# Two squared-ReLU MLPs in float32: block products by Strassen's algorithm in place of plain tiles

## The chip, the cores and the metric

One core of a Trainium2 chip runs the whole kernel in one launch. The metric is the time of one execution on the device, in microseconds (us). Of the kernel before there are three timed runs, and one more execution that was profiled.

## The reference

A decoder trunk of two layers on 1024 tokens of 1024 features, all in float32. Each layer has a mixer (layer 0: sparse attention beside a short convolution; layer 1: latent attention) and then an MLP, each inside two normalisations and a residual. The change concerns the MLP alone:

```python
x = x + rms_norm(mixer(rms_norm(x, g_mix_pre)), g_mix_post)
h = rms_norm(x, g_ffn_pre)                 # [1024 tokens, 1024]
u = jnp.square(jax.nn.relu(h @ w1))        # w1 [1024, 4096]
x = x + rms_norm(u @ w2, g_ffn_post)       # w2 [4096, 1024]
```

## The kernel before

**Products.** Every product is float32, made of three matmuls on rounded parts: a value v is split into hi, its copy in the rounded type fp32r (ScalarE, L258), and lo = v - hi (a subtraction on VectorE or GpSimd, L261). `mm3` (L266 to L269) then adds hi·hi, hi·lo and lo·hi into one PSUM region. So each product of two 128-row tiles has three matmuls, lines L267, L268 and L269, each 128 x 128 weights against up to 512 columns.

**Memory.** SBUF is cut into 25 pages of 8 KB per partition (class `Mem`, L35), from which all large tiles come; a tile that finds no page waits until another is freed. PSUM has two pools of two-bank tiles, `psS` (two buffers of [128, 1024]), and one-bank tiles, `psM` (three) and `psO` (one).

**Order.** The program is written in one thread of Python. A scheduler orders the instructions of TensorE, VectorE (DVE), ScalarE (ACT) and GpSimd (POOL) by its own estimate of when each is ready and how urgent it is; each engine then runs its list strictly in that order on the chip. SyncE (SP) issues the loads in the order of the program.

**Into the MLP.** `OutProj` (L781) multiplies a mixer's output by its projection, one block of 128 tokens at a time; `rest` (L824) adds the residual (L324, L325) and makes the next normalised block `xn` (L312). Two program steps later `put` (L834) gives it to `HN.put` (L336), which transposes it on TensorE (L341) and splits the transposed block into hi and lo. So the MLP's input is stored split, feature-major, before the MLP begins; `finish` (L840) does that for the last block. `Stream` (L271) loads and splits the weights of the MLP in tiles of [128, 1024] (512 KB), each tile once.

**The MLP** (`mlp`, L1105). The 4096 feed-forward columns are taken in 16 chunks of 256. For each chunk, `up` (L1111) makes two 128-column tiles for each half of the tokens: 8 row tiles of `w1` times 3 matmuls of 512 columns into a `psM` bank, then ReLU on ACT (L1118), the square on DVE (L1119) and the split into `at`. `down` (L1126) multiplies the chunk before by its rows of `w2` for each of the 8 token blocks into a `psS` tile of 1024 columns, and DVE adds it into the accumulator in SBUF (L1144). In the last chunks `down` takes two chunks at once and calls of a `tail` stand between its blocks: `tail0` (layer 0) normalises each finished block and starts layer 1's first projections (the `wd` products); `tail1` (L1470, layer 1) does the last residual row by row and writes the output. `tail1` calls the last block with `halves`, which evacuates its two halves apart (L1138), and finishes that row in halves (L1485 to L1493).

Of the kernel before, what the change touches and what calls it, by code (L numbers as in the profile page):

```python
# [21 lines left out]
P = 128  # L22
S = 1024
D = 1024
# [10 lines left out]
class Mem:  # L35
    """Pages of SBUF of 8 KB per partition; each serves tiles of one type, in quarters."""
# [96 lines left out]
def hybrid_kernel(ctx: ExitStack, tc: tile.TileContext, x, pos, g_mix_pre, g_mix_post, g_ffn_pre, g_ffn_post,  # L133
# [103 lines left out]
    def rope(eng, v, tb, off, n):  # L237
        """Rotates v [P, ..., 2n] of token block tb in place; off is where its table starts."""
# [32 lines left out]
    class Stream:  # L271
        """Weights in order of use: loads run ahead, then each is split into its parts."""
# [47 lines left out]
    def residual(src, tb, gain, xt, x_out, eng=None, queue=None):  # L320
        """x + rms(src) * gain of token block tb."""
# [8 lines left out]
    class HN:  # L330
        """Normalised activations, feature-major, in two parts."""
# [25 lines left out]
    # =========================================================== layer 0: mixer  # L357
# [88 lines left out]
    # start: normalise, transpose, first indexer chunk  # L446
# [19 lines left out]
    # key and weight columns of the indexer, feature-major, then token-major  # L466
# [314 lines left out]
    class OutProj:  # L781
        """Token-major product with weights [1024, 1024], residual and the next normalised activations;
        lhs_src(tb) gives the pieces of its transposed left side."""

        def __init__(self, weights, lhs_src, gpost, gpre, x_in, x_out, done, follow):
# [3 lines left out]
            self.hn, self.s, self.l, self.lag = HN(), {}, {}, []  # L789
# [15 lines left out]
        def product(self, tb):  # L805
# [6 lines left out]
            if tb == NB - 2:  # L812
                self.follow.load(2)
# [10 lines left out]
        def rest(self, tb):  # L824
# [3 lines left out]
            if tb >= NB - 1:  # L828
                self.follow.step(2 // 1)
# [717 lines left out]
```

## Time and profile before

| | us |
|---|---|
| median of three timed runs (lowest, highest) | 2734.79 (2731.08, 2738.48) |
| the profiled execution's own time: span from its first to its last instruction | 2734.3 |
| TensorE busy | 2654.1 (97%) |
| DVE busy | 1496.3 (55%) |
| ACT busy | 1112.1 (41%) |
| POOL busy | 824.5 (30%) |
| the six groups of MLP matmuls, 1024 each | 6144 matmuls |

The profile has six parts: busy time by engine; the span in 40 slices with the TensorE clock that was granted; the DMA queues; the chain of work that ended last; the costliest groups of instructions; and the DMA issues. The trace behind it can be asked for the instructions of one engine in order of time (the timeline), for tables of busy time by stretch (windows) and for groups by line. "Releaser" is what ended an engine's wait. A matmul's listed duration (389 ns) contains time in which the next one already runs, so the pace of matmuls is read from how many fit into a stretch.

### The profile page before, as it was taken

How to read it: one execution, taken by the hardware profiler on the slowest of the kernel's cores; microseconds unless marked ns; L12 is line 12 of the kernel's file. 1: busy time of each engine (PE TensorE's matmuls, PEld its weight loads, DVE VectorE, ACT ScalarE, POOL GpSimd, SP SyncE). 2: the span in 40 equal slices, each digit the busy share in tenths (PEclk: the TensorE clock that was granted, in tenths of full speed). 3: DMA queues.
4: the chain of work that ended last, by engine and by line, in shares of the span. 5: the costliest groups of instructions: out<-in, count | busy, mean ns of one | idle time of the engine just before them, and what ended most of it. 6: DMA issues, size and time to landing. Idle time of an engine off the chain costs nothing. (4 is left out here: it accounts for less than half of the span.)

```text
span 2734.3 us, 34579 instructions
## 1 busy us (share of the span) xinstructions
PE 2654.1 (97%) x13496; PEld 2214.3 (81%) x13496; DVE 1496.3 (55%) x2559; ACT 1112.1 (41%) x2107; POOL 824.5 (30%) x819
## 2 busy tenths in 40 slices
PE   7999999999999999999999999999999999999998
PEld 6887799766888888888888987777888888888887
DVE  5668999466543433333345478888652433433344
ACT  5554453576442212121224557888543222212122
POOL 4663255543022212122222233334112222222122
PEclk9999999999999999999999999999999999999999
DMA  3001110003421110111123341111331111110103
GB/s 113 24 32 47 62 63 17 1 1 111 136 77 54 39 62 31 62 48 46 54 77 108 127 156 52 34 47 48 108 116 54 41 53 54 39 62 31 62 31 131
DMA packets 67587, 171.58 MB, mean 63 GB/s; under 512 B 5904, under 2 KB 29968, under 8 KB 67424
## 3 DMA queue, kind: packets, MB, share of 16 engines
q1 hardware_dynamic: 60624, 145.19, 15.6%
q0 software_dynamic: 6656, 23.93, 2.3%
q8 instruction: 106, 1.74, 0.3%
q14 instruction: 57, 0.47, 0.1%
q10 hardware_dynamic: 144, 0.26, 0.0%
HBM read 138.95 MB, written 30.41 MB: 62 GB/s over the span
## 5 line engine op out<-in xcount | busy, mean ns | idle before, releaser
L261 POOL TENSOR_TENSOR w<-raw,w 128x1024 fp32r<-128x1024 f32 x128 | 307.4, 2401 | 1019.3 <-ACT w L258 1014.2
L1144 DVE TENSOR_TENSOR acc<-psS,acc 128x1024 f32<-128x1024 f32 x223 | 273.0, 1224 | 410.9 <-PE psS L269 410.4
L269 PE MATMUL psS<-w,at 128*128 128x512 f32 x1024 | 398.0, 389 | 2.1 <-DVE at L261 2.1
L267 PE MATMUL psS<-w,at 128*128 128x512 f32 x1024 | 398.8, 389 | 1.2 <-DVE acc L1138 0.8
L267 PE MATMUL psM<-hn,w 128*128 128x512 f32 x1024 | 398.5, 389 | 0.0
L268 PE MATMUL psS<-w,at 128*128 128x512 f32 x1024 | 398.4, 389 | 0.0
L269 PE MATMUL psM<-hn,w 128*128 128x512 f32 x1024 | 398.4, 389 | 0.0
L268 PE MATMUL psM<-hn,w 128*128 128x512 f32 x1024 | 398.3, 389 | 0.0
L258 ACT ACTIVATE w<-raw 128x1024 fp32r<-128x1024 f32 x132 | 139.7, 1059 | 618.3 <-PE psS L269 584.4
L1119 DVE SCALAR_TENSOR_TENSOR raw<-psM,raw 128x512 f32<-128x512 f32 x120 | 83.0, 691 | 302.4 <-ACT raw L1118 302.4
L269 PEld LDWEIGHTS psS<-w,at 128*128 128x128 f32 x1024 | 192.1, 188 | 42.8 <-DVE at L261 3.0
L267 PEld LDWEIGHTS psS<-w,at 128*128 128x128 f32 x1024 | 192.2, 188 | 41.7 <-DVE acc L1138 1.2
L268 PEld LDWEIGHTS psM<-hn,w 128*128 128x128 f32 x1024 | 192.2, 188 | 39.9
L269 PEld LDWEIGHTS psM<-hn,w 128*128 128x128 f32 x1024 | 192.2, 188 | 39.9
L268 PEld LDWEIGHTS psS<-w,at 128*128 128x128 f32 x1024 | 192.2, 188 | 39.7
L267 PEld LDWEIGHTS psM<-hn,w 128*128 128x128 f32 x1024 | 192.1, 188 | 39.8
L882 POOL TENSOR_SCALAR pr<-pr,tot 128x896 f32<-128x896 f32 (+7 forms) x181 | 133.5, 744 | 227.1 <-DVE tot L881 187.5
L1118 ACT ACTIVATE raw<-psM 128x512 f32<-128x512 f32 x120 | 71.8, 598 | 285.9 <-PE psM L269 285.9
L261 DVE TENSOR_TENSOR at<-raw,at 128x512 fp32r<-128x512 f32 x120 | 136.2, 1135 | 86.0 <-ACT at L258 86.0
L267 PE MATMUL psM<-wh,hn 128*128 128x256 f32 x576 | 159.3, 293 | 13.3 <-ACT tok L655 10.3
L269 PE MATMUL psM<-wh,hn 128*128 128x256 f32 x576 | 156.2, 288 | 0.0
L268 PE MATMUL psM<-wl,hn 128*128 128x256 f32 x552 | 150.4, 289 | 1.8 <-POOL wl L261 1.8
(707 smaller groups left out, 5509.0 us busy)
## 6 DMA issues: line engine op xcount, KB each, us to landing
raw<-in_w SPq DMA_DIRECT2D x128, 512.0 KB, 3.9
xt<-xs_d SPq DMA_DIRECT2D x15, 512.0 KB, 4.1
qtok<-q_d SPq DMA_DIRECT2D x8, 896.0 KB, 5.0
q_d<-qstage POOLq DMA_DIRECT2D x28, 224.0 KB, 2.6
xs_d<-xn POOLq DMA_DIRECT2D x12, 512.0 KB, 3.0
raw<-in_w_qkv SPq DMA_DIRECT2D x10, 512.0 KB, 4.2
xn<-in_x SPq DMA_DIRECT2D x9, 512.0 KB, 4.4
v_d<-vt POOLq DMA_DIRECT2D x8, 512.0 KB, 2.9
```

The costliest lines, as they stand in the source:

```text
L258: nc.scalar.activation(hi, src, AF.Copy)
L261: (lo_eng or nc.vector).tensor_tensor(lo, src, f(hi), op=ALU.subtract)
L267: nc.tensor.matmul(dst, lh, rh, start=start, stop=False)
L268: nc.tensor.matmul(dst, lh, rl, start=False, stop=False)
L269: nc.tensor.matmul(dst, ll, rh, start=False, stop=stop)
L882: nc.gpsimd.tensor_scalar(pt_, pt_, tot, 1.0, op0=ALU.mult, op1=ALU.mult)
L1118: nc.scalar.activation(r, m, AF.Relu)
L1119: nc.vector.scalar_tensor_tensor(r, m, 0.0, r, op0=ALU.max, op1=ALU.mult)
L1144: nc.vector.tensor_tensor(dst, s_, dst, op=ALU.add)
```

## The change

**What it does.** The 4096 columns are taken in four groups of 1024. In a group both products, up (tokens x features times features x columns) and down (tokens x columns times columns x features), are 1024 x 1024 x 1024, and each is cut into 2 x 2 blocks of 512 x 512. Seven products of sums and differences of blocks (the Winograd form of Strassen's algorithm) take the place of the eight plain block products. A block product n is 4 column tiles j by 4 contraction tiles q by 3 matmuls (L1277). Each of the 56 block products of a layer is a step: 4 groups of 7 up steps (order n = 1, 2, 6, 5, 7, 3, 4) and 7 down steps (n = 1, 5, 6, 3, 7, 2, 4). Steps alternate between two sets of four PSUM banks (three `psM` and `psO`; the two `psS`). Sums of products are kept by adding a later product into the same banks, and most products are evacuated in between.

The sums of blocks are formed in float32 on DVE by `comb` (L1109, 128 x 2048), and every combined block is split anew by `parts`: hi on ACT (L1102, two halves of 1024), lo (L1103, two halves) on POOL or DVE, by the table in `left` and `right`. So the MLP's input is not split by `put` any more: `Blocks` stores it transposed in float32 (copies L372). The seven splits of the MLP's input are made in group 0, on DVE, stored to DRAM by SP and read back for groups 1 to 3. The weights come in 1 MB tiles of [128, 2048]. The preparation of a step stands one step ahead of its product in the program. In the last step (n = 4 of the last down) each column tile j completes token block 4 + j; the halved last row of `tail1` is now evacuated whole.

```diff
@@ class Blocks, takes the place of HN in OutProj
+            for kh in range(2):
+                m = big[:, kh * 512:(kh + 1) * 512] if last else psM()
+                for i in range(4):
+                    nc.tensor.transpose(m[:, i * P:(i + 1) * P], xn[:, (kh * 4 + i) * P:(kh * 4 + i + 1) * P], idf)
...
+                nc.scalar.activation(self.t[kh, th][:, :, c * P:(c + 1) * P], m.rearrange("p (a b) -> p a b", b=P),
+                                     AF.Copy)
@@ OutProj.rest
-            if tb >= NB - 1:
-                self.follow.step(2 // 1)
+            if tb == NB - 1:
+                self.follow.prep(0)
@@ class Mlp
+        UP, DOWN = (1, 2, 6, 5, 7, 3, 4), (1, 5, 6, 3, 7, 2, 4)
...
+        def parts(self, v, lo_eng, keep=False):
+            hi, lo = mem([P, 2048], F32R, "hi"), mem([P, 2048], F32R, "lo")
+            for i, eng in enumerate(lo_eng):
+                c = slice(i * 1024, (i + 1) * 1024)
+                nc.scalar.activation(hi[:, c], v[:, c], AF.Copy)
+                eng.tensor_tensor(lo[:, c], v[:, c], f(hi[:, c]), op=ALU.subtract)
...
+        def left(self, kind, g, n):
+            if kind == "up":
+                r, lo = self.w1, (nc.gpsimd, nc.gpsimd)
+            else:
+                r, lo = self.h, (nc.vector, nc.gpsimd)
...
+        def right(self, kind, g, n):
+            if kind == "up" and g:
+                return self.tq.pop((g, n))
+            if kind == "up":
+                lo = (nc.vector, nc.vector)
+                r = self.x
...
+                elif n == 6:
+                    t3 = r["t3"] = mem([P, 2048], F32, "t3")
+                    t2 = r["t2"] = mem([P, 2048], F32, "t2")
+                    self.comb(t3, r[1, 1], r[0, 1], sub)
+                    self.comb(t2, t3, r[0, 0], add)
+                    res = self.parts(t2, lo, True)
...
+            r, lo = self.w2, (nc.gpsimd, nc.gpsimd)
...
+        def loads(self, s):
+            if kind == "up" and g == 0 and GROUPS > 1:
+                (hi, lo) = self.ready[s][1]
+                nc.sync.dma_start(self.td[n - 1, :, 0:2048], f(hi))
+                nc.sync.dma_start(self.td[n - 1, :, 2048:4096], f(lo))
+            k2, g2, n2, i2 = self.steps[s + 2] if s + 2 < len(self.steps) else (None,) * 4
+            if k2 == "up" and g2:
+                t = mem([P, 2048], F32R, "th"), mem([P, 2048], F32R, "tl")
+                for h in range(2):
+                    nc.sync.dma_start(f(t[h]), self.td[n2 - 1, :, h * 2048:(h + 1) * 2048])
+                self.tq[g2, n2] = t
+            if i >= 3:
+                if kind == "up":
+                    self.load(self.w2, w2, g, *order[i - 3])
+                elif g + 1 < GROUPS:
+                    self.load(self.w1, w1, g + 1, *order[i - 3])
...
+        def product(self, s, js=range(4)):
+            for j in js:
+                for q in range(4):
...
+                    for m, (l, r) in enumerate(((sh, th), (sh, tl), (sl, th))):
+                        nc.tensor.matmul(bank[j], l[:, a], r[:, b], start=new and q == 0 and m == 0,
+                                         stop=q == 3 and m == 2, skip_group_check=True)
...
+        def evac(self, s, js=None):
+            if kind == "up":
+                for sl_, b in units:
+                    if n == 4:
+                        nc.scalar.activation(d, b, AF.Relu)
+                        v.scalar_tensor_tensor(d, b, 0.0, d, op0=ALU.max, op1=ALU.mult)
+                    elif new:
+                        nc.scalar.activation(d, b, AF.Copy)
+                    else:
+                        v.tensor_tensor(d, b, d, op=ALU.add)
+                        v.scalar_tensor_tensor(d, d, 0.0, d, op0=ALU.max, op1=ALU.mult)
...
+                else:
+                    v.tensor_tensor(at, b, at, op=ALU.add)
...
+        def run(self, finish):
+            for s in range(last):
+                self.prep(s + 1)
+                self.loads(s)
+                self.product(s)
+                if s == 0:
+                    finish()
+                self.evac(s)
@@ tail1
-        d = down(NB - 1, True)
+        d = down(NB - 1)
```

**How the order moves.** In the rows below, names carry buffer and version numbers; left of the arrow stands what is written, right of it what is read (of a matmul the moving operand first). The first place is DVE where the MLP of layer 0 begins. Here `xn` is the residual of the last token block, `psS_623` the last product of the output projection, `hn` or `xb` the MLP's input, `at` an activation. Before:

```order
L324 SCALAR_TENSOR_TENSOR xn_1078_6865<-psS_623_6961,rs_627_7035,gp_987_6280 128x1024
L261 TENSOR_TENSOR w1_1099_7029<-raw_1081_6874,w1_1099_7029 128x1024
L325 TENSOR_TENSOR xn_1078_6865<-xn_1078_6865 128x1024
L1119 SCALAR_TENSOR_TENSOR xn_1104_7041<-psM_630_7052,xn_1104_7041 128x512
L261 TENSOR_TENSOR at_1111_7079<-xn_1104_7041,at_1111_7079 128x512
L306 RECIPROCAL rs_629_7044<-rs_629_7044 128x1
L312 SCALAR_TENSOR_TENSOR xn_1104_7041<-xn_1078_6865,rs_629_7044,gp_987_6280 128x1024
L1119 SCALAR_TENSOR_TENSOR xn_1104_7041<-psM_631_7087,xn_1104_7041 128x512
L261 TENSOR_TENSOR at_1111_7079<-xn_1104_7041,at_1111_7079 128x512
```

And now (`lo_1097` is the lo part of the first right operand, which the first block product reads; the rows of `xn` are the same work as before):

```order
L312 SCALAR_TENSOR_TENSOR xn_1088_6945<-xn_1062_6766,rs_622_6948,gp_987_6281 128x1024
L324 SCALAR_TENSOR_TENSOR xn_1074_6853<-psS_623_6952,rs_627_7027,gp_987_6281 128x1024
L1103 TENSOR_TENSOR lo_1097_7020<-xb_1026_6493,hi_1096_7019 128x1024 x2
L325 TENSOR_TENSOR xn_1074_6853<-xn_1074_6853 128x1024
L306 RECIPROCAL rs_629_7036<-rs_629_7036 128x1
L312 SCALAR_TENSOR_TENSOR xn_1100_7033<-xn_1074_6853,rs_629_7036,gp_987_6281 128x1024
```

The split that the first product needs came from blocks split earlier, one block at a time; now it is made whole, behind the residual row of the last block.

The second place is the same engine a little later, up to the operand of the third step (n = 6). `psS_635` and `psS_636` are the two halves of the second step (n = 2), `t3` and `t2` the sums of input blocks, `lo_1116` the lo part of `t2`, which step n = 6 multiplies. Before, in the same place:

```order
L1119 SCALAR_TENSOR_TENSOR raw_1115_7085<-psM_634_7130,raw_1115_7085 128x512
L261 TENSOR_TENSOR at_1122_7157<-raw_1115_7085,at_1122_7157 128x512
L1119 SCALAR_TENSOR_TENSOR raw_1115_7085<-psM_635_7165,raw_1115_7085 128x512
L261 TENSOR_TENSOR at_1122_7157<-raw_1115_7085,at_1122_7157 128x512
L1119 SCALAR_TENSOR_TENSOR raw_1137_7201<-psM_636_7203,raw_1137_7201 128x512
L261 TENSOR_TENSOR at_1139_7230<-raw_1137_7201,at_1139_7230 128x512
```

And now:

```order
L1109 TENSOR_TENSOR raw_1078_6864<-raw_1078_6864,s2_1110_7123 128x2048
L1308 TENSOR_TENSOR h_1109_7118<-psS_635_7143,h_1109_7118 128x1024
L1109 TENSOR_TENSOR t3_1113_7131<-xb_1070_6842,xb_1069_6835 128x2048
L1309 SCALAR_TENSOR_TENSOR h_1109_7118<-h_1109_7118 128x1024
L1109 TENSOR_TENSOR t2_1114_7132<-t3_1113_7131,xb_1026_6493 128x2048
L1109 TENSOR_TENSOR xb_1069_6835<-xb_1069_6835,xb_1026_6493 128x2048
L1308 TENSOR_TENSOR h_1109_7118<-psS_636_7144,h_1109_7118 128x1024
L1103 TENSOR_TENSOR lo_1132_7274<-t3_1113_7131,hi_1131_7273 128x1024
L1309 SCALAR_TENSOR_TENSOR h_1109_7118<-h_1109_7118 128x1024
L1103 TENSOR_TENSOR lo_1132_7274<-t3_1113_7131,hi_1131_7273 128x1024
L1103 TENSOR_TENSOR lo_1116_7136<-t2_1114_7132,hi_1115_7135 128x1024 x2
```

Before, each row waits for one bank and serves the next; now the sums and splits for n = 6 stand behind two rows (L1308) that wait for the product n = 2. On TensorE the transposes of the last token block (`xn_1104` before, `xn_1100` now) stood together; this is TensorE before:

```order
L269 MATMUL psS_638_7267<-w2_1113_7082,at_1111_7079 128x512
L269 MATMUL psS_639_7281<-w2_1113_7082,at_1111_7079 128x512
L341 MATMUL psM_632_7116<-idf_77,xn_1104_7041 128x128 x4
L341 MATMUL psM_633_7123<-idf_77,xn_1104_7041 128x128 x4
L267 MATMUL psS_638_7267<-w2_1125_7160,at_1111_7079 128x512
```

And now, where the other four transposes stand ahead of the whole product n = 2:

```order
L1277 MATMUL psS_635_7143<-lo_1105_7048,hi_1102_7040 128x512
L1277 MATMUL psS_635_7143<-hi_1104_7047,lo_1103_7041 128x512
L369 MATMUL psS_634_7107<-idf_77,xn_1100_7033 128x128 x4
L1277 MATMUL psS_636_7144<-hi_1104_7047,hi_1102_7040 128x512
L1277 MATMUL psS_636_7144<-lo_1105_7048,hi_1102_7040 128x512
```

The last four, which complete the block that `t3` reads, now stand between the two halves of n = 2.

The third place is POOL: before, in the steady part of layer 0; now, in a down set of the second group; `raw` are weight blocks or sums of them, `s1` and `h` sums of activations and activations, `w1` and `w2` weight tiles. Before:

```order
L261 TENSOR_TENSOR w1_1159_7387<-raw_1143_7236,w1_1159_7387 128x1024
L261 TENSOR_TENSOR w1_1162_7391<-raw_1154_7356,w1_1162_7391 128x1024
L261 TENSOR_TENSOR w2_1170_7482<-raw_1154_7356,w2_1170_7482 128x1024
L261 TENSOR_TENSOR w2_1181_7602<-raw_1164_7394,w2_1181_7602 128x1024
L261 TENSOR_TENSOR w1_1188_7636<-raw_1172_7485,w1_1188_7636 128x1024
L261 TENSOR_TENSOR w1_1191_7640<-raw_1183_7605,w1_1191_7640 128x1024
```

And now:

```order
L1103 TENSOR_TENSOR lo_1267_8496<-raw_1241_8232,hi_1266_8495 128x1024 x2
L1103 TENSOR_TENSOR lo_1265_8489<-s1_1263_8486,hi_1264_8488 128x1024
L1103 TENSOR_TENSOR lo_1272_8562<-raw_1241_8232,hi_1271_8561 128x1024 x2
L1103 TENSOR_TENSOR lo_1270_8555<-s1_1263_8486,hi_1269_8554 128x1024
L1103 TENSOR_TENSOR lo_1278_8631<-raw_1254_8361,hi_1277_8630 128x1024 x2
L1103 TENSOR_TENSOR lo_1275_8625<-s1_1263_8486,hi_1274_8624 128x1024
L1103 TENSOR_TENSOR lo_1283_8689<-h_1221_8086,hi_1282_8688 128x1024
L1103 TENSOR_TENSOR lo_1286_8695<-raw_1249_8297,hi_1285_8694 128x1024 x2
L1103 TENSOR_TENSOR lo_1299_8820<-h_1243_8284,hi_1298_8819 128x1024
```

Before, one split of 128 x 1024 for each weight tile; now two for each weight operand of a step and one for each activation operand.

## Rows read from the trace of the kernel before

**Rows 1.** The profile, part 1: span, and busy time by engine.

```profile
span 2734.3 us, 34579 instructions
...
PE 2654.1 (97%) x13496; PEld 2214.3 (81%) x13496; DVE 1496.3 (55%) x2559; ACT 1112.1 (41%) x2107; POOL 824.5 (30%) x819
```

**Rows 2.** Windows in layer 0's MLP: length, busy time (instructions), clock, DMA share, GB/s.

```profile
863.00:963.00 100.00, 100.00 (x443) 82.81 (x442) 38.79 (x38) 20.19 (x27) 21.56 (x9) 1.00 0.12 42
...
763.00:1418.00 655.00, 653.93 (x2891) 541.13 (x2890) 251.35 (x242) 151.16 (x206) 148.33 (x66) 1.00 0.14 50
1418.00:1540.00 122.00, 119.01 (x695) 109.81 (x694) 70.65 (x145) 58.73 (x168) 31.83 (x60) 0.99 0.34 117
```

**Rows 3.** The profile, part 5: groups with count, busy time, mean ns, idle before.

```profile
L261 POOL TENSOR_TENSOR w<-raw,w 128x1024 fp32r<-128x1024 f32 x128 | 307.4, 2401 | 1019.3 <-ACT w L258 1014.2
L1144 DVE TENSOR_TENSOR acc<-psS,acc 128x1024 f32<-128x1024 f32 x223 | 273.0, 1224 | 410.9 <-PE psS L269 410.4
...
L267 PE MATMUL psM<-hn,w 128*128 128x512 f32 x1024 | 398.5, 389 | 0.0
...
L258 ACT ACTIVATE w<-raw 128x1024 fp32r<-128x1024 f32 x132 | 139.7, 1059 | 618.3 <-PE psS L269 584.4
```

**Rows 4.** POOL's timeline: start, us, line, operation, idle before.

```profile
1031.51 2.40 POOL L261 TENSOR_TENSOR w<-raw,w 128x1024 fp32r<-128x1024 f32 x1 [19.36 <-ACT w L258]
1034.26 2.39 POOL L261 TENSOR_TENSOR w<-raw,w 128x1024 fp32r<-128x1024 f32 x1 [0.35 <-ACT w L258]
```

**Rows 5.** DVE's timeline, the same columns.

```profile
1012.95 0.69 DVE L261 TENSOR_TENSOR at<-raw,at 128x512 fp32r<-128x512 f32 x1 [0.70 <-ACT at L258]
...
1033.27 0.69 DVE L1119 SCALAR_TENSOR_TENSOR raw<-psM,raw 128x512 f32<-128x512 f32 x1 [1.67 <-ACT raw L1118]
1034.73 2.46 DVE L261 TENSOR_TENSOR at<-raw,at 128x512 fp32r<-128x512 f32 x1 [0.77 <-ACT at L258]
```

**Rows 6.** TensorE's timeline where layer 0's MLP begins.

```profile
762.27 0.40 PE L269 MATMUL psS<-wo,lhs 128*128 128x512 f32 x1
762.50 1.04 PE L341 MATMUL psM<-idf,xn 128*128 128x128 f32 x8
763.29 0.47 PE L267 MATMUL psM<-hn,w 128*128 128x512 f32 x1
```

**Rows 7.** DVE's timeline at the same place.

```profile
765.73 1.28 DVE L324 SCALAR_TENSOR_TENSOR xn<-psS,rs,gp 128x1024 f32<-128x1024 f32 x1
766.93 1.22 DVE L261 TENSOR_TENSOR w<-raw,w 128x1024 fp32r<-128x1024 f32 x1
```

**Rows 8.** TensorE's timeline, two waits.

```profile
107.78 0.67 PE L426 MATMUL psM<-idr,qx 128*128 128x128 f32 x4 [4.06 <-POOL qx L419]
...
310.07 0.47 PE L267 MATMUL psS<-hn,w 128*128 128x512 f32 x1 [2.36 <-DVE raw L624]
```

**Rows 9.** Windows of 5 us around these waits, and one in layer 0's last chunk.

```profile
105.00:110.00 5.00, 2.21 (x9) 2.02 (x10) 2.31 (x3) 1.09 (x2) 2.56 (x3) 0.80 0.00 0
110.00:115.00 5.00, 5.00 (x34) 4.72 (x33) 3.36 (x4) 2.33 (x3) 0.00 (x0) 0.86 0.02 3
...
310.00:315.00 5.00, 4.93 (x22) 4.13 (x23) 4.93 (x10) 1.35 (x3) 0.00 (x0) 1.00 0.00 2
...
1460.00:1465.00 5.00, 5.00 (x22) 5.00 (x21) 3.50 (x8) 2.56 (x6) 1.93 (x7) 0.69 0.60 213
```

**Rows 10.** Timelines of DVE, POOL and TensorE at the end of layer 1.

```profile
2717.29 1.28 DVE L324 SCALAR_TENSOR_TENSOR xt<-acc,rs,gp 128x1024 f32<-128x1024 f32 x1
...
2728.49 1.42 DVE L1491 SCALAR_TENSOR_TENSOR tt<-acc,rs,gp 128x512 f32<-128x512 f32 x2
2729.83 1.28 DVE L1492 TENSOR_TENSOR xt<-xt,tt 128x512 f32<-128x512 f32 x2
...
2718.65 2.40 POOL L325 TENSOR_TENSOR xt<-xt,xt 128x1024 f32<-128x1024 f32 x1 [2.98 <-DVE xt L324]
...
2725.87 0.39 PE L269 MATMUL psS<-w,at 128*128 128x512 f32 x1
```

More of the change, by code (lines that the diff above doesn't have):

```diff
@@ L355, in free, with __init__, put @@
             free(*self.t.values())
+    class Blocks:
+        def __init__(self):
+            self.t = {}
+        def put(self, tb, xn, last=False):
+            th, c = divmod(tb, 4)
+            big = psS() if last else None
+            for kh in range(2):
+                m = big[:, kh * 512:(kh + 1) * 512] if last else psM()
+                for i in range(4):
+                    nc.tensor.transpose(m[:, i * P:(i + 1) * P], xn[:, (kh * 4 + i) * P:(kh * 4 + i + 1) * P], idf)
+                if (kh, th) not in self.t:
+                    self.t[kh, th] = mem([P, 4, 512], F32, "xb")
+                nc.scalar.activation(self.t[kh, th][:, :, c * P:(c + 1) * P], m.rearrange("p (a b) -> p a b", b=P),
+                                     AF.Copy)
     hn = HN()
@@ L788, in __init__ @@
             self.done, self.follow = done, follow
-            self.hn, self.s, self.l, self.lag = HN(), {}, {}, []
+            self.hn, self.s, self.l, self.lag = Blocks(), {}, {}, []
         def lhs(self, tb):
@@ L812, in product @@
             if tb == NB - 2:
-                self.follow.load(2)
+                self.follow.begin(self.hn.t)
             l = self.l.pop(tb)
@@ L1050, in hybrid_kernel @@
     hn.free()
[L1051 to L1074 removed]
+    GROUPS = 4
@@ L1076, in free_cat @@
+    def mlp_weights(layer):
+        return Mlp(layer)
     def free_cat(tb):
@@ L1105, in mlp @@
     def mlp(op, tail):
-        st, hn_, finish = op.follow, op.hn, op.finish
-        w1p, w2p = st.w1p, st.w2p
-        acc = [mem([P, 2, D], F32, "acc") for _ in range(4)]
-        at_ = {}
-        def up(c, th, jj):
-            j = 2 * c + jj
-            m = psM()
-            for kt in range(8):
-                mm3(m, w1p[j][:, 0, kt], w1p[j][:, 1, kt], hn_.half(0, kt, th), hn_.half(1, kt, th),
-                    kt == 0, kt == 7)
-            r = mem([P, 512], F32, "r")
-            nc.scalar.activation(r, m, AF.Relu)
-            nc.vector.scalar_tensor_tensor(r, m, 0.0, r, op0=ALU.max, op1=ALU.mult)
-            t = at_[c, th, jj] = mem([P, 2, 512], F32R, "at")
-            split(r, t[:, 0], t[:, 1])
-            free(r)
-            if th:
-                free(w1p.pop(j))
@@ L1152, in mlp @@
-        for c in range(NC):
-            last = c == NC - 1
-            up(c, 0, 0)
-            st.step(1)
-            up(c, 0, 1)
-            if c == 0:
-                finish()
-            if c and not last:
-                for tb in range(4):
-                    down([c - 1], tb)
-            up(c, 1, 0)
-            st.step(1)
-            up(c, 1, 1)
-            st.step(2)
-            if c and not last:
-                for tb in range(4, 8):
-                    down([c - 1], tb)
@@ L1169, in mlp @@
-        hn_.free()
-        tail(lambda tb, halves=False: down([NC - 2, NC - 1], tb, halves), acc)
+        m = op.follow
+        m.run(op.finish)
+        tail(m.row, m.acc)
     qa = {}
```

233 lines of the change are left out of this document (183 added, 50 removed).

## The prediction

> **What bounds the kernel now.** I read the busy times first: TensorE works 2654.1 of 2734.3 us, DVE 55%, POOL 30% [rows 1]. That is a share of the whole, so next come the windows inside one MLP: in 655 us of layer 0's MLP TensorE is busy for 653.93, at clock 1.00, with DVE at 251 and POOL at 148 [rows 2]. The groups say the same of the waits: the MLP's up matmuls have no idle time before them, while DVE and POOL idle most of the time, waiting for TensorE or ACT [rows 3]. In the MLP the number of matmuls is the time. Their pace: 443 in 100 us [rows 2], 0.226 us each (the listed 389 ns overlap the next one). Layer 1's MLP has the same groups, which count both layers.
>
> **Removed.** Six groups of 1024 matmuls, one of them shown [rows 3], become 2 layers x 56 block products x 48 = 5376, all of 512 columns. 6144 - 5376 = 768, times 0.226 = **-173.6 us**. A block product takes 48 x 0.226 = 10.9 us and a set of seven 76; everything below asks whether the operands of the next one are there every 10.9 us.
>
> **Added beside TensorE.** The splits on POOL go from 128 to 280 of the same shape (2.40 us [rows 3]): 14 in an up set, 21 in a down set. DVE gets 104 sums of 128 x 2048. None exists in the trace; DVE rows of 512 columns take 0.69 and of 1024 take 1.22 [rows 3, 5], so 0.53 per 512 and 2.29 for 2048. These sums read two operands in SBUF, and the timelines show what that means beside POOL. POOL ran a split from 1034.26 to 1036.65 [rows 4]; DVE's split of two SBUF operands at 1034.73 took 2.46, its end 0.54 after POOL's, where the same operation alone took 0.69 [rows 5]. A DVE row that reads PSUM took 0.69 at 1033.27, inside POOL's split that began at 1031.51 [rows 4, 5]. So POOL and DVE's two-SBUF work add up, and evacuations do not. I take it as working in both directions. The sum per set:
> - down: 21 x 2.40 + 8 sums x 2.29 + 7 DVE splits x 1.22 = 77 of 76 us available;
> - up, groups 1 to 3: 14 x 2.40 + 4 x 2.29 + the squares on DVE (4 x 1.28 + 4 x 0.69) = 51 of 76;
> - up, group 0, where DVE splits the input as well: 51 + 4 x 2.29 + 14 x 1.22 = 77 of 76.
>
> Of a layer's 608 us this is 3 x 51 + 5 x 77 = 538. It fits, but with little air in five of eight sets. Within a down set it is uneven: three steps with two sums each need 3 x 2.40 + 2 x 2.29 + 1.22 = 13.0 us against 10.9, the others 8.4 to 10.7. In the DVE order sums and splits stand one to two products ahead of their use, so an excess of 3 x 2.1 = 6.4 us should mostly be carried by that lead. I take 1.5 us for each of the 8 down sets, between 0 and 6.4: **+12**. For the uneven up sets of group 0 (the steps with three sums need 14.1) 5 each, between 0 and 10: **+10**.
>
> ACT gets 364 splits of 1.06 us [rows 3], 386 us in 1216 us of MLP, and stays far from the bound: nothing. `Blocks` drops a split per block and keeps a copy: nothing.
>
> **Start of each MLP.** Today the first matmul of the MLP follows the last transposes without a gap (762.50, 763.29) [rows 6]. Now three hi·hi matmuls and the transposes can run, some 1.7 us after the last projection matmul (762.27 + 0.40), to about 764.4. Then `lo_1097` is wanted, which stands behind L324 of the last block: that runs at 765.73, and what follows it at 766.93 takes 1.22 [rows 7], so the first half is there at 768.1. A wait of 3.7, say 4 (2.5 to 6), in both layers: **+8**.
>
> **Operand of the third step, n = 6.** This is the largest term after the matmuls. On DVE its last link stands behind two rows (L1308) that wait for halves of n = 2, and `t3` needs the transposes that TensorE runs between those halves. From the start of n = 2: 24 matmuls 5.4, add 1.22, `t3` 2.29, square 1.28, `t2` 2.29, a sum 2.29, add 1.22, split 1.22, square 1.28, split 1.22, first half of `lo_1116` 1.22: 20.9 us. TensorE has 10.9 of product and half of the 1.04 of transposes [rows 6]: 11.4. The wait is 9.5, if POOL keeps out. POOL has four splits to run in that time; if each gets in ahead of a sum, it is 9.5 + 9.6 = 19.1. I take half, 14.3.
>
> After a wait that long the clock counts. Behind a wait of 4.06 us [rows 8] the granted clock was 0.80 and then 0.86 in the next 5 us, while 2.36 us left it at 1.00 [rows 8, 9]. These are means between the levels 2.4 and 1.2 GHz, so 0.20 and 0.14 of 5 us were lost, 1.7 us together. So 16 us a layer (11 to 21): **+32**.
>
> **Tails.** In `tail0` the last product completes four blocks in its last 11 us instead of one every few us, and layer 1's projections need them normalised. The old stretch has 3 us of idle TensorE in 122 [rows 2], as much cover as a shift can find. I take **+4** (0 to 15). In `tail1` rows 4 to 7 become complete during the last product. Today the span ends 8.4 us after the last matmul's start (2725.87) [rows 1, 10]. Now six POOL adds of 2.40 and seven DVE rows of 1.28 [rows 10] are one serial stretch with the last row's 1.42 + 1.28 [rows 10] and an add of 1.22: 27 us, beginning about 5.6 before that product starts and followed by the 3 us of the output transfer. That ends 25 us after the product's start, 14 after its end: 5 later than today, **+5** (0 to 12).
>
> **Sum.** -173.6 + 12 + 10 + 8 + 32 + 4 + 5 = -102.6. From the profiled span of 2734.3, which is 0.5 below the median of the runs, that is 2631.7; as a time **2632 us**. With every added term at its low end it is about 2588 (5 + 22 left of the terms), at the high end about 2713 (51 + 20 + 12 + 42 + 15 + 12 = 152).
>
> **Rivals.**
> - *The waits are hidden.* POOL may stay out of the n = 6 chain and the down sets may run on their lead. For it: POOL is in order and may wait for ACT at that moment. Then 2 x 2.5 + 2 x 9.5 + 2 x 1.7 is left, some 28: about 2589.
> - *The lead is not there.* If an in-order row on DVE waits for an evacuation just when a sum is due, each step pays its own excess: 6.4 per down set and 10 per first up set, 51 + 20 in place of 12 + 10, or 49 more: about 2681. For it: 77 of 76 leaves no room to catch up. Against it: the up sets of groups 1 to 3 have 25 us of slack each, to begin a down set ahead.
> - *Transfers are late.* In groups 1 to 3, 24 up steps read 2.1 MB of stored operands and 1.05 MB of weights. At the fastest window here, 213 GB/s [rows 9], 3.15 MB take 14.8 us, 3.9 more than a product: 24 x 3.9 = 94, about 2726. Against it: that window used 0.60 of the DMA engines. The Trainium skill ("SBUF — State Buffer", section "SBUF: two separate sides") gives the DMA side 436 GB/s; an estimate from that page is 7.2 us for the 3.15 MB, so no wait and 2632. No run here shows such a rate.
> - *Slower: the clock falls again and again.* If the lock starves not a few but many products, each long wait costs twice, as at 107.78: 4.06 idle and 1.7 at the low clock [rows 8, 9], 5.8 us. The gain of 173.6 less the other terms (8 + 32 + 4 + 5 = 49) is gone after 125 / 5.8 = 22 such waits in 112 products. Candidates are the 24 down steps that need 13.0 us, and two in the first up sets (n = 5). If all 26 wait like that, the time is 2734.8 - 125 + 151 = about 2761. Against it: their own excess is 2.1 to 3.2 us, and 2.36 us left the clock alone. The Trainium skill ("TensorE: Matmul & The Clock Gate", section "HAM oscillation — how this bites in real kernels") describes the case: a loop whose tile computes for less time than it waits starts every tile at the low clock. By that rule a product of 10.9 us that waits 2 to 3 us keeps its clock; the wait of 2.36 us above agrees.
> - That the change does not do what it says is out: the new order has 5376 matmul rows of L1277.
>
> **How the numbers follow.** My forecast (2600 to 2655) gets 0.52. Hidden waits (below 2600) get 0.15, the missing lead (2655 to 2710) 0.24, late transfers 0.04, the falling clock 0.05. The range takes in the first three: 2586 to 2702. I call a difference beyond 0.3% (8 us) one that can be told from no change. Faster is 0.52 + 0.15 + 0.24 and half of the late transfers, 0.93; the other half lands within 0.3%, 0.02; slower 0.05.
>
> **What would show it.** The groups should list L1277 with 5376 matmuls at the same pace. TensorE's timeline should have one wait of some 14 us in the first up set of each layer, ahead of the third product, ended by DVE's L1103, with a lower clock behind it. The other steps of groups 1 to 3 should follow each other without gaps above 2 us. POOL should be busy for about 1200 us (152 more splits of 2.40), and DVE's L1109 should average well above 2.29. From the last matmul to the end should be 13 to 14 us. I am wrong if TensorE waits in most down steps (the missing lead), if its waits are ended by DMA (transfers), or if the clock in the steady groups is below 1.00.

## The result, and the profile after

The changed kernel takes **2618.84 us** in the median of four runs (2615.92 to 2621.27); the kernel before took 2736.17 in four runs beside it (2731.08 to 2738.48). The ratio is 0.957, with a 95% interval of 0.956 to 0.959: 117 us less, inside the stated range and 13 us below the forecast of 2632. The profiled execution took 2619.16 us, of which its span is 2617.4.

The first parts of the profile of the changed kernel, to be held against [rows 1, 3]:

```profile
span 2617.4 us, 33623 instructions
...
PE 2499.7 (96%) x12728; PEld 2079.4 (79%) x12728; DVE 1753.4 (67%) x2534; ACT 1250.2 (48%) x2203; POOL 1335.4 (51%) x975
...
L1103 POOL TENSOR_TENSOR lo<-raw,hi 128x1024 fp32r<-128x1024 f32 x208 | 585.1, 2837 | 282.0 <-ACT hi L1102 220.5
...
L1109 DVE TENSOR_TENSOR raw<-raw,raw 128x2048 f32<-128x2048 f32 x40 | 100.5, 2514 | 30.9 <-DMA raw<-in_w 30.9
```

TensorE is busy for 154 us less and is still the bound. POOL and DVE work much more, and the means show that they hold each other up (the prediction's "POOL and DVE's two-SBUF work add up"; what they share is called the port below): 2837 ns for a split that took 2401 before, 2514 for a sum whose median is 2284. The list of the instructions of L1277 has 18 groups, of which two are:

```profile
L1277 PE MATMUL psS<-hi,hi x608: 389/389/792, 784.5 to 2601.5; 128*128 128x512 f32 x152
...
L1277 PE MATMUL psM<-th,hi x288: 389/389/389, 939.6 to 2518.1; 128*128 128x512 f32 x144
```

With the others they add up to 5376. Windows of the changed kernel: most of the first set of layer 0, then two stretches as long as a set from the steady part, in which DVE and POOL prepare a down set and then an up set, then three of 5 us (length; busy times of TensorE, its weight loads, DVE, ACT and POOL; clock, DMA share, GB/s):

```profile
760.00:840.00 80.00, 63.80 (x259) 50.51 (x258) 55.98 (x34) 35.69 (x47) 45.17 (x17) 0.85 0.54 214
...
986.00:1062.00 76.00, 76.00 (x337) 62.94 (x336) 69.59 (x43) 30.82 (x35) 57.42 (x20) 1.00 0.16 55
...
1062.00:1138.00 76.00, 76.00 (x337) 62.90 (x337) 23.68 (x16) 19.06 (x23) 41.11 (x17) 1.00 0.65 249
...
800.00:805.00 5.00, 3.11 (x6) 1.66 (x6) 5.00 (x3) 5.00 (x6) 4.83 (x2) 0.50 0.32 133
...
810.00:815.00 5.00, 5.00 (x18) 3.93 (x18) 3.79 (x3) 1.11 (x2) 3.27 (x1) 0.73 1.01 415
...
825.00:830.00 5.00, 5.00 (x24) 4.14 (x23) 0.00 (x0) 2.58 (x3) 5.00 (x3) 1.00 1.03 434
```

In the steady part TensorE never waits, though DVE is busy for 70 of 76 us while a down set is prepared. The count of 337 takes in matmuls that are cut by the window's ends; from the start of one product to the start of the next, 48 matmuls, it is 10.88 us (863.48 to 874.36, for one), 0.2267 each. In the first window TensorE is busy for 64 of 80 us, at a clock of 0.85. Four marks on TensorE's timeline cut the span into stretches. Before (with 762.27 [rows 6] and 2725.87 [rows 10]):

```profile
1538.03 0.29 PE L269 MATMUL psS<-wd,lhs 128*128 128x288 f32 x1
...
2024.01 0.39 PE L269 MATMUL psS<-wo,lhs 128*128 128x512 f32 x1
```

And after:

```profile
761.66 0.39 PE L269 MATMUL psS<-wo,lhs 128*128 128x512 f32 x1
...
1475.82 0.29 PE L269 MATMUL psS<-wd,lhs 128*128 128x288 f32 x1
...
1962.51 0.39 PE L269 MATMUL psS<-wo,lhs 128*128 128x512 f32 x1
...
2601.95 0.39 PE L1277 MATMUL psS<-hi,lo 128*128 128x512 f32 x1
```

| stretch | before, us | after, us | difference |
|---|---|---|---|
| to layer 0's last projection matmul | 762.3 | 761.7 | -0.6 |
| layer 0's MLP and the `wd` products | 775.8 | 714.2 | -61.6 |
| layer 1's mixer | 486.0 | 486.7 | +0.7 |
| layer 1's MLP | 701.9 | 639.4 | -62.4 |
| from the last matmul to the end | 8.4 | 15.4 | +7.0 |

384 matmuls less are some 87 us a layer. So some 25 us came back in each layer, and 7 at the end. Nearly all of the 25 lies in the first up set. TensorE's waits there, in layer 0:

```profile
769.29 1.09 PE L369 MATMUL psM<-idf,xn 128*128 128x128 f32 x4 [7.02 <-DVE xn L312]
...
801.83 1.65 PE L1277 MATMUL psM<-hi,hi 128*128 128x512 f32 x3 [4.77 <-ACT hi L1102]
...
808.24 0.80 PE L1277 MATMUL psM<-lo,hi 128*128 128x512 f32 x1 [3.30 <-DVE lo L1103]
```

With the small ones they are 16.2 us in layer 0 and 13.4 in layer 1. In the windows behind them the clock stands at 0.50, the lower level. Busy time times what the clock lacks, summed over windows of 5 us, is an estimate of 7 us lost in layer 0 and 9 in layer 1. DVE's timeline shows what the first wait was for:

```profile
760.24 2.28 DVE L1109 TENSOR_TENSOR s<-raw,raw 128x2048 f32<-128x2048 f32 x1
762.44 1.22 DVE L325 TENSOR_TENSOR xn<-xn 128x1024 f32<-128x1024 f32 x1
763.58 2.29 DVE L1109 TENSOR_TENSOR raw<-s,raw 128x2048 f32<-128x2048 f32 x1
766.88 0.35 DVE L306 RECIPROCAL rs<-rs 128x1 f32<-128x1 f32 x2 [1.02 <-ACT rs L305]
767.14 2.00 DVE L312 SCALAR_TENSOR_TENSOR xn<-xn,rs,gp 128x1024 f32<-128x1024 f32 x1
```

Two sums of weight blocks, wanted only for the third and fourth product, ran ahead of the normalisation (L325, L312) of the last block but one. POOL's split of the first sum began at 763.75 and took 4.31 us in place of 2.40: it had to let DVE's second sum end first. So POOL also waits for DVE.

### The profile page after: what moved, and what is told of

The parts are those of the page before. It is cut to its first block, busy times and chain, and to the rows that moved or that the text cites. A ratio compares the mean times of both kernels' runs of the same rounds, so it can differ in the third digit from the quotient of the medians.

```text
span 2617.4 us, 33623 instructions
## 1 busy us (share of the span) xinstructions
PE 2499.7 (96%) x12728; PEld 2079.4 (79%) x12728; DVE 1753.4 (67%) x2534; ACT 1250.2 (48%) x2203; POOL 1335.4 (51%) x975
## 4 chain that ended last, share of the span: by engine, by line
PE 73%; DVE 13%; issue 5%; ACT 4%; POOL 2%; DMA 2%; POOLq 0%; SPq 0%; DVEq 0%; ACTq 0%
PE psS L1277 22%; PE psM L1277 17%; PE psO L1277 6%; PE psM L928 3%; DVE mask L699 3%; PE psM L267 2%; PE psM L268 2%; PE psM L269 2%; PE psS L269 2%; PE psS L267 2%; PE psS L268 2%; PE psO L915 2%; PE psO L916 2%; DVE mask L696 1%; PE psS L1059 1%
## 5 line engine op out<-in xcount | busy, mean ns | idle before, releaser
L1103 POOL TENSOR_TENSOR lo<-raw,hi 128x1024 fp32r<-128x1024 f32 x208 | 585.1, 2837 | 282.0 <-ACT hi L1102 220.5
L1102 ACT ACTIVATE hi<-raw 128x1024 fp32r<-128x1024 f32 x208 | 208.0, 1052 | 362.2 <-PE psS L1277 232.3
L1277 PE MATMUL psS<-hi,hi 128*128 128x512 f32 x608 | 239.5, 395 | 5.6 <-DVE acc L1322 4.2
L1277 PE MATMUL psS<-lo,hi 128*128 128x512 f32 x608 | 237.9, 391 | 0.0
L1277 PE MATMUL psS<-hi,lo 128*128 128x512 f32 x608 | 237.6, 391 | 0.0
L1103 POOL TENSOR_TENSOR lo<-s,hi 128x1024 fp32r<-128x1024 f32 x40 | 125.5, 3145 | 161.2 <-ACT hi L1102 94.5
L1277 PE MATMUL psM<-hi,hi 128*128 128x512 f32 x384 | 153.8, 403 | 10.2 <-ACT hi L1102 10.2
L1277 PE MATMUL psM<-lo,hi 128*128 128x512 f32 x384 | 152.8, 398 | 7.3 <-DVE lo L1103 7.3
L1102 ACT ACTIVATE hi<-s 128x1024 fp32r<-128x1024 f32 x64 | 64.3, 1053 | 194.7 <-DVE s L1109 194.7
L1277 PE MATMUL psM<-hi,lo 128*128 128x512 f32 x384 | 151.9, 396 | 0.0
L898 ACT ACTIVATE pr<-pr,nm 128x896 f32<-128x896 f32 (+7 forms) x181 | 136.7, 756 | 23.7 <-DVE pr L894 11.1
L1277 PEld LDWEIGHTS psS<-hi,hi 128*128 128x128 f32 x608 | 115.1, 190 | 31.6 <-DVE acc L1322 5.0
L928 PE MATMUL psM<-idf,pr 128*128 128x128 f32 x788 | 130.3, 276 | 5.2 <-DVE pt L261 1.9
L1277 PEld LDWEIGHTS psS<-hi,lo 128*128 128x128 f32 x608 | 115.0, 189 | 24.1
L1277 PEld LDWEIGHTS psS<-lo,hi 128*128 128x128 f32 x608 | 115.0, 189 | 23.8
L1308 DVE TENSOR_TENSOR h<-psS,h 128x1024 f32<-128x1024 f32 x32 | 39.1, 1222 | 139.3 <-PE psS L1277 139.3
L1109 DVE TENSOR_TENSOR raw<-raw,raw 128x2048 f32<-128x2048 f32 x40 | 100.5, 2514 | 30.9 <-DMA raw<-in_w 30.9
```

The lines of the kernel that those rows point to most:

```text
L898: nc.scalar.activation(pt_, pt_, AF.Exp, bias=nm, scale=-1.0, accum_out=tot)
L928: nc.tensor.transpose(m[:, i * P:(i + 1) * P], u["p"][4 * g + i0 + i][:, kb * P:(kb + 1) * P], idf)
L1102: nc.scalar.activation(hi[:, c], v[:, c], AF.Copy)
L1103: eng.tensor_tensor(lo[:, c], v[:, c], f(hi[:, c]), op=ALU.subtract)
L1109: (eng or nc.vector).tensor_tensor(out, a, b, op=op)
L1277: nc.tensor.matmul(bank[j], l[:, a], r[:, b], start=new and q == 0 and m == 0, stop=q == 3 and m == 2, skip_group_check=True)
```

## The experiments

Theory S says that the rest of the price lies in the order of DVE's rows at the start of each MLP. Rival L says that the port shared by POOL and DVE sets the pace there. Two further questions are how much lead the steady sets have, and what the end costs. The kernel before took 2738 to 2739 us beside these runs, so the changed kernel's ratio makes 2622 there. Traces are compared by the stretches of the table, since the code ahead of the first mark, where it is the same, ended between 761.4 and 766.8 us from run to run. The waits of a first set differ from trace to trace as well: where the code of that set is the changed kernel's (down_lo_pool, down_sums_pool, tail_preload, tail_dve) they are 16.2 to 18.3 us in layer 0 and 16.6 to 16.9 in layer 1, against the changed kernel's 16.2 and 13.4.

**sums_behind.** In group 0 the sum `s2` multiplies one operand by a 1.0 that is made from a statistic of the last block (`r` in `residual`), so it can't run ahead of that row.

```diff
+            nc.vector.tensor_scalar(one, r, 0.0, 1.0, op0=ALU.mult, op1=ALU.add)
...
-                    self.comb(s2, r[1, 1], r[1, 0], sub)
+                    if g == 0:
+                        nc.vector.scalar_tensor_tensor(s2, r[1, 1], self.one, r[1, 0], op0=ALU.mult, op1=ALU.subtract)
+                    else:
+                        self.comb(s2, r[1, 1], r[1, 0], sub)
```

> The sum s2 of weight blocks in the first group (and the two sums made from it) is tied to the last token block's residual, so that DVE can't run it ahead of the normalisation of the last blocks. Theory S (what is left of the price sits in the order of DVE at the start of each layer's MLP, and in the clock behind the waits): TensorE's wait of 7.02 us for xn in layer 0 falls below 3 us, layer 1 loses some 2 us; the time falls by 5 to 11 us. Rival L (the start set is bound by the port that POOL and DVE share: 77 us of such work in 76): the same work only moves, waits come up at the second to fifth product, and the time stays within 4 us.

2623.19 us, ratio 0.959 (0.957 to 0.961): no gain. TensorE's waits in layer 0:

```profile
773.01 1.94 PE L371 MATMUL psM<-idf,xn 128*128 128x128 f32 x8 [2.69 <-DVE xn L312]
...
793.38 1.12 PE L371 MATMUL psS<-idf,xn 128*128 128x128 f32 x4 [7.01 <-DVE xn L312]
```

The first wait fell from 7.02 to 2.69 as S said, and a wait of 7.01 came up one block later, where the sums now stood ahead of the last block's L312. The waits of the set are 18.9 us against 16.2, and 18.0 against 13.4 in layer 1. This speaks for L.

**last_block_early.** The last block's transposes use two PSUM tiles, and `finish` is called ahead of the first product.

```diff
-            big = psS() if last else None
...
-                m = big[:, kh * 512:(kh + 1) * 512] if last else psM()
+                m = psS()[:, :512] if last else psM()
...
+                if s == 0:
+                    finish()
                 self.product(s)
-                if s == 0:
-                    finish()
```

> The transposes of the last token block go to two PSUM tiles ahead of the first product in the program; in the new order DVE makes t3, t2 and the split for n = 6 ahead of the two rows that wait for product n = 2. Theory S: the two waits ahead of n = 6 (4.77 and 3.30 us in each layer) fall to under 3 us together, and the clock behind them comes back: 14 to 24 us less for both layers. Rival L: the same lock work, waits move to n = 5 and n = 7, the time changes by less than 5 us.

2598.06 us, ratio 0.949 (0.947 to 0.951): 24 us less than the changed kernel, as S said. The MLP stretches are 703.8 and 625.9. Ahead of n = 6 one wait of 1.07 us is left in layer 0, and the start still has its own:

```profile
776.20 1.94 PE L368 MATMUL psM<-idf,xn 128*128 128x128 f32 x8 [7.04 <-DVE xn L312]
...
805.07 0.50 PE L1276 MATMUL psM<-lo,hi 128*128 128x512 f32 x1 [1.07 <-DVE lo L1102]
```

The waits of the set fell by 7.0 and 6.5 us, the stretches by 10.4 and 13.5. The rest, 10.4 us in all, is about what the clock gave back: by the same windows it now costs 2 and 4 us in the two sets, in place of 7 and 9.

**both_starts.** The two edits together.

> Both edits together. Theory S: the gains add, 18 to 34 us less, and the first set of each layer runs with under 6 us of waits. Rival L: under 6 us less.

2603.21 us, ratio 0.951 (0.948 to 0.953): 19 us less than the changed kernel, at the low end of what S expected, but no better than last_block_early alone. The waits are 11.3 and 8.8 us where S expected less than 6, over 8 of them in each layer again ahead of the last block's transposes.

**sums_after_last.** As both_starts, with the 1.0 made from the normalised last block.

```diff
         nc.vector.scalar_tensor_tensor(xn, xt, r, gain, op0=ALU.mult, op1=ALU.mult)
+        if one is not None:
+            nc.vector.tensor_scalar(one, xn[:, 0:1], 0.0, 1.0, op0=ALU.mult, op1=ALU.add)
```

> The two edits of both_starts, with s2 tied to the normalised last block itself instead of its residual, so that no sum of weights can stand ahead of the last block's L312 either. Theory S (the order of DVE makes the waits): the waits ahead of the last block's transposes (8.27 and 8.24 us in both_starts) fall below 4 us, no new wait above 3 us elsewhere in the set: 6 to 14 us less than both_starts, 2590 to 2597 us where the kernel before takes 2739. Rival L (the shared port sets the pace of the start set): another wait of 4 us or more comes up at n = 6 or later and the time stays within 4 us of both_starts.

2602.7 us, ratio 0.951 (0.949 to 0.953). The waits are 10.0 and 8.2 us: no longer in one place, but nearly the same sum. The time is that of both_starts, as L said and S did not, though L's wait of 4 us at n = 6 is not there either (the longest of that kind is 3.35). Wherever the weight sums stand, 7 to 11 us a layer stay. S holds for n = 6, whose operand really stood behind the wrong rows, and fails for the sums.

**group0_lo_dve.** last_block_early, and less work on the shared port in the first set.

```diff
-                r, lo = self.w1, (nc.gpsimd, nc.gpsimd)
+                r, lo = self.w1, (nc.gpsimd, nc.gpsimd) if g else (nc.vector, nc.vector)
```

> last_block_early, and in group 0 the lo parts of the weights are split on DVE (1.22) instead of POOL (2.40): 14 x 1.18 = 17 us less shared-port work in that set (60 of 76 us), but 17 us more in DVE's queue, some of it ahead of the last blocks' rows. Rival L (the shared port sets the pace of the start set): the waits in each start set (9.2 and 6.9 us in last_block_early) fall below 4 us, 8 to 15 us less in all. Theory S (the order of DVE's rows makes the waits): the rows ahead of the last blocks' L312 grow by two splits, the waits stay or grow, 0 to 8 us more.

2589.89 us, ratio 0.946 (0.944 to 0.947), 8 us less than last_block_early by the ratios. The waits fell from 9.2 to 5.9 and from 6.9 to 4.7 us, though more splits stand ahead of the last blocks. DVE's residual row of the last block, first in last_block_early and then here, and the wait that is left in layer 0:

```profile
782.59 3.42 DVE L325 TENSOR_TENSOR xn<-xn 128x1024 f32<-128x1024 f32 x1
```

```profile
769.48 1.22 DVE L325 TENSOR_TENSOR xn<-xn 128x1024 f32<-128x1024 f32 x1
```

```profile
766.25 1.94 PE L368 MATMUL psM<-idf,xn 128*128 128x128 f32 x8 [5.64 <-DVE xn L312]
```

With POOL out of the way DVE's rows are no longer held up. So the port is part of that price, as L said, and its gain is at the lower end of what L expected. L's waits below 4 us were not reached: the 5.64 us are for an L312 that stands behind two sums and two splits, which is S's part. early_lo_tail below repeats it with 6.1 and 5.1 us, against 9.2 and 7.6 in early_and_tail.

**down_lo_pool.** How much more the steady sets would bear.

```diff
-                r, lo = self.h, (nc.vector, nc.gpsimd)
+                r, lo = self.h, (nc.gpsimd, nc.gpsimd)
```

> In the down sets both halves of the activation's lo part go to POOL (28 POOL splits of 2.40 and no DVE split, 7 x 1.18 = 8 us more lock work in a set: 85 us in 76). Theory S (a lead from the up sets carries it: 51 us of 76 there): no change, within 4 us. Rival L (each set pays its own excess): 8 to 9 us more in each of 8 down sets, 60 to 75 us slower.

2641.41 us, ratio 0.964 (0.963 to 0.966): 19 us slower than the changed kernel, between the two. At the end of each of a layer's first three down sets TensorE now waits 1.45 to 2.38 us, and for an evacuation, not for an operand. DVE and POOL there:

```profile
1075.49 18.55 DVE L1109 TENSOR_TENSOR raw<-raw,raw 128x2048 f32<-128x2048 f32 x1 [3.31 <-POOL lo L1103]
1093.96 1.21 DVE L1322 TENSOR_TENSOR acc<-psS,acc 128x1024 f32<-128x1024 f32 x1
```

```profile
1072.98 18.91 POOL L1103 TENSOR_TENSOR lo<-raw,hi 128x1024 fp32r<-128x1024 f32 x8
```

A sum of 2.28 us took 18.55, until POOL had finished the last of eight splits that followed each other without a pause. The evacuation L1322 stood behind it, and TensorE waited 2.35 us for the bank. Here POOL kept the port while seven more splits went by. The same sum took 17.2 to 18.6 us in six of the eight down sets, each time ahead of one of these waits.

**down_sums_pool.** A much larger excess.

```diff
-            (eng or nc.vector).tensor_tensor(out, a, b, op=op)
+            (eng or self.ceng).tensor_tensor(out, a, b, op=op)
...
+            self.ceng = nc.gpsimd if kind == "down" else nc.vector
```

> In the down sets the eight sums go from DVE (2.29 us) to POOL (twice that, about 4.6): 21 x 2.4 + 8 x 4.6 + 7 x 1.22 = 96 us of shared-port work in 76, and POOL alone 87. Full lead (a down set may run up to 25 us behind, the slack of the up set before it): no change. Lead of about 7 us, as down_lo_pool suggests (excess 9, paid 2.4 a set): 20 - 7 = 13 us in each of 8 sets, some 100 us slower. No lead: 160 us slower.

2786.7 us, ratio 1.018 (1.016 to 1.020): slower than the kernel before by 1.8%, and 165 us slower than the changed kernel, as without any lead (160). In each down set TensorE waits several times. The longest wait of the second one in layer 0, and the window of 5 us around it (columns as above):

```profile
1066.95 0.80 PE L1278 MATMUL psS<-hi,lo 128*128 128x512 f32 x1 [8.87 <-POOL lo L1103]
```

```profile
1065.00:1070.00 5.00, 3.05 (x7) 2.48 (x8) 2.26 (x1) 3.52 (x4) 5.00 (x2) 0.50 0.00 0
```

A sum took 4.5 to 4.6 us on POOL. Behind the first up sets TensorE's waits are 116 us in all, and the windows put some 42 us more down to the clock (an estimate). So nearly all of the 20 us of excess was paid in every set, some of it as lost clock: the lead does not grow to the 25 us of slack of the up sets.

**tail_preload** and **tail_dve.** The residual rows of the end are loaded ahead; in the second the adds go to DVE too.

```diff
+        rows = [load_res(xs_d[2], tb) for tb in range(NB)]
-            xt = load_res(xs_d[2], tb)
+            xt = rows[tb]
...
-        xt = load_res(xs_d[2], NB - 1)
+        xt = rows[NB - 1]
```

```diff
-            last = (d, tb, gp, xt, out, nc.gpsimd)
+            last = (d, tb, gp, xt, out, nc.vector)
```

> The eight residual rows of the end are loaded before the last product in the program, not one by one behind the output rows on SP's queue. If the late load of the last row (issued at 2608.38, wait of 1.87 us) and its row behind the seventh add set the end: from the last matmul to the end 2 to 3 us less than 15.5. Rival: DVE's chain ends as late anyway, less than 1 us.

> tail_preload, and the adds of the rows on DVE (1.22) instead of POOL (2.40). Theory: POOL's adds block DVE's rows through the shared port (3.24 and 3.37 us for rows of 1.28, 2.29 for one of 0.15) and so keep a PSUM bank from the last product (wait of 2.68 us): the wait goes, and the end comes 4 to 8 us earlier than in the changed kernel. Rival: DVE's own work (8 rows x 3.3 us) is as long as the shared work it replaces: within 2 us of tail_preload.

In the changed kernel DVE's timeline at the end reads:

```profile
2593.71 3.37 DVE L324 SCALAR_TENSOR_TENSOR xt<-acc,rs,gp 128x1024 f32<-128x1024 f32 x1
...
2605.64 2.29 DVE L1700 TENSOR_TENSOR rs<-ssl 128x1 f32<-128x1 f32 x1
...
2612.91 1.29 DVE L1705 TENSOR_TENSOR xt<-xt,tt 128x512 f32<-128x512 f32 x2 [1.87 <-DMA xt<-xs_d]
```

and TensorE's:

```profile
2597.74 0.68 PE L1277 MATMUL psS<-hi,hi 128*128 128x512 f32 x1 [2.68 <-DVE acc L1322]
```

A row of 1.28 and a sum of one column were held up by POOL's adds, a bank came back 2.68 us late, and the last row's load came late. With the loads ahead, the end after the last matmul fell from 15.4 to 13.0 us, as expected; the time, 2618.73 (ratio 0.956, 0.955 to 0.958), hardly tells it. With the adds on DVE the wait was gone and the end was 12.4: 2612.53 us, ratio 0.954 (0.953 to 0.956), about 8 less, the upper end of the theory's 4 to 8.

**early_and_tail** (last_block_early and tail_dve), **all_starts_tail** (sums_after_last, the diff of group0_lo_dve, and tail_dve) and **early_lo_tail** (group0_lo_dve and tail_dve).

> last_block_early and tail_dve together. They touch different stretches, so the gains should add: 24 and 8 us against the changed kernel, 2586 to 2594 us where the kernel before takes 2739. If less than 25 us, one of the two gave its gain to a later wait.

> sums_after_last (sums of weights behind the last block, transposes ahead of the first product), the weights' lo parts of group 0 on DVE, and tail_dve. If both matter, the order and the port: waits of the start sets below 5 us (10.0 and 8.2 in sums_after_last), 8 to 18 us less than early_and_tail, 2572 to 2584 us. If the port does not matter there: like early_and_tail within 5 us. If DVE itself is the bound of that set (its queue 60 of 76 us, but all of it behind the last block): waits move to n = 6 and n = 5 and the time is equal or up to 10 us more.

> group0_lo_dve and tail_dve together, the edits that each gained. If they add as early_and_tail did: 8 us less than group0_lo_dve (2590 where the kernel before takes 2739), 2579 to 2585 us; start sets with 5.9 and 4.7 us of waits, no wait in the last product, 12 to 13 us from the last matmul to the end.

2589.31 us, ratio 0.946 (0.944 to 0.947): the two gains add, 32 us less than the changed kernel by the ratios. all_starts_tail took 2598.2, ratio 0.948 (0.947 to 0.950), and has its waits back at n = 6:

```profile
796.94 1.65 PE L1283 MATMUL psM<-hi,hi 128*128 128x512 f32 x3 [4.71 <-ACT hi L1105]
...
805.16 0.79 PE L1283 MATMUL psM<-lo,hi 128*128 128x512 f32 x1 [4.88 <-DVE lo L1106]
```

Everything stands behind the last block there, and DVE's rows follow each other from 778.56 to 812.98 us with less than 0.7 us of idle: its queue is the bound, the third of the cases expected. early_lo_tail took 2587.29, ratio 0.946 (0.944 to 0.947). Its trace is the shortest, with stretches of 698.4 and 618.0 us and an end of 12.4, but its five runs spread over 13 us, and its median lies 2 us above what was expected, so it can't be told from early_and_tail. Both beat the kernel before by over 5% and the changed kernel by over 1%.

## Why the prediction was right, and where it was not

- **Removed, -173.6.** Right: 5376 matmuls at 0.2267 us, and full windows in all steady sets.
- **Down sets +12 and uneven up sets +10.** Measured 0: between 815 and 1390 us TensorE has no wait, nor between 2015 and 2595. The lead covers the unevenness, as the text thought it mostly would; I charged 22 us for a chance. The rival of the missing lead was wrong for this kernel. It was near: with 85 us of port work in a down set of 76 (down_lo_pool) the time is 19 us longer, with 96 (down_sums_pool) 165.
- **Start, +8.** Mis-reasoned, though the size, 12.0 us of waits for both layers, is not far off. The waits on the way into the first product are 7.4 us in layer 0 and 2.7 in layer 1, with 1.9 more ahead of the last block's transposes. They were nearly all for L312, behind weight sums; `lo_1097`, which I named, cost 0.42 and 0.27. I had read the rows behind L324 of the last block, not those ahead of it.
- **n = 6, +32.** The place and the releaser (DVE's L1103, and ACT's split ahead of it) were right, and moving the rows took the wait away. The sizes were off in both directions. The waits are 8.1 us and not 14.3, since POOL held DVE up by 3 us in that chain and not by 4.8, TensorE had 3 us of work between the two waits, which the sum left out, and the second half of n = 2 started late. The clock cost 7 and 9 us in the two sets, not 1.7 each. I had priced it from a wait of 4.06 us that left a clock of 0.80 and 0.86; here whole windows stand at 0.50. That this term and the start together came near (45 us for 40) is luck: the wait was put 6 us too long in each layer and the clock 5 to 7 us too low.
- **Tails, +4 and +5.** The end took 7.0 more and a wait of 2.68 in the last product, some 10 us in all. The serial stretch of POOL and DVE was the cause, as described. `tail0` fits: what the waits and the clock of the first set don't explain in layer 0 is about 2 us.
- **The other rivals.** No wait of TensorE in the MLPs was ended by a transfer. The windows reach 434 GB/s at a share of 1.03, where I had bounded them by 213 at 0.60. The Trainium skill ("SBUF — State Buffer", section "SBUF: two separate sides") gives the DMA side 436 GB/s, and the trace agrees. The falling clock came in the first set of a layer and not in the others; down_sums_pool shows that the rival was real, with 0.50 and 0.58 in the windows of 5 us around the wait of 8.87 and a time above the kernel before. There too the waits themselves cost more than the clock behind them, 116 us and some 42.

So the total came out 13 us too high: 22 us of price were not there and `tail0` cost 2 us less, while the start sets cost about 45 us in place of 40 and the end 10 in place of 5.

## What to carry to other kernels

When work that an engine does for the steady state also floats into the start, read what stands ahead of the rows that the next stage waits for, not only what stands behind them. Two engines that share a port need a count of their joint work and a look at the longest run of ready instructions on either: a run of eight held the other for nearly all of it here, and the evacuation queued behind the victim stopped TensorE. Waits of several us cost a third to two thirds of their length again in clock here (7 us for 16, 9 for 13, and 42 for 116 in down_sums_pool, by estimate), so removing one is worth more than its length.

## What had not been expected of the hardware

The port is not always passed on when the holder's instruction ends. Mostly it is. In the changed kernel 115 of DVE's rows with two SBUF operands were held up, none of them by more than 2.3 us, about one split. DVE and POOL take turns there, though each has its next instruction ready:

```profile
1024.32 4.39 DVE L1109 TENSOR_TENSOR h<-h,h 128x2048 f32<-128x2048 f32 x1
1028.63 3.44 DVE L1103 TENSOR_TENSOR lo<-s,hi 128x1024 fp32r<-128x1024 f32 x1
```

```profile
1018.74 7.81 POOL L1103 TENSOR_TENSOR lo<-raw,hi 128x1024 fp32r<-128x1024 f32 x2
1026.51 4.47 POOL L1103 TENSOR_TENSOR lo<-s,hi 128x1024 fp32r<-128x1024 f32 x1
```

The 18.55 us of down_lo_pool are an exception, and POOL suffered another in the changed kernel, while DVE ran a sum and two splits behind each other (1964.44 to 1968.99):

```profile
1964.56 10.01 POOL L1103 TENSOR_TENSOR lo<-s,hi 128x1024 fp32r<-128x1024 f32 x2 [4.92 <-ACT hi L1102]
```

Two splits of 2.40 took 10.01 us, the first alone 6.68. What makes an engine keep the port past its turn is not shown. The Trainium skill ("SBUF — State Buffer", section "SBUF: two separate sides") says that the pair is locked for a whole instruction and the other engine blocks; the trace agrees, and shows in addition that a wait can outlast several instructions.

The clock does not follow the length of a wait alone. In down_lo_pool four waits of the same kind and nearly the same length left different clocks; TensorE's rows, and the windows behind them:

```profile
1095.23 0.50 PE L1277 MATMUL psS<-hi,hi 128*128 128x512 f32 x1 [2.35 <-DVE acc L1322]
...
2306.58 0.50 PE L1277 MATMUL psS<-hi,hi 128*128 128x512 f32 x1 [2.35 <-DVE acc L1322]
```

```profile
1095.20:1100.20 5.00, 4.97 (x15) 3.94 (x16) 4.90 (x6) 0.34 (x1) 0.00 (x0) 0.66 0.00 0
...
2306.50:2311.50 5.00, 4.92 (x21) 4.05 (x22) 4.90 (x7) 0.29 (x1) 0.00 (x0) 1.00 0.01 3
```

After 2.35 us the clock was 0.66 once and 1.00 once; the other two waits, of 2.38 us, left 1.00 (at 1251.92) and 0.66 (at 2461.78). No length alone tells them apart, so the rule that I drew from the Trainium skill ("TensorE: Matmul & The Clock Gate", section "HAM oscillation — how this bites in real kernels"), that a product of 10.9 us keeps its clock through such a wait, agrees with the trace in two of four cases. The section's own case is the opposite one, a tile that computes for less time than it waits. And my sentence that 2.36 us leave it alone [rows 8, 9] was one sample of two outcomes, and part of the spread between runs of the same kernel may come from there: in early_lo_tail the run with a mean clock of 0.993 took 2578.43 us, the one with 0.987 took 2591.24. That this is the cause was not tried.
